# A diffusion backbone on one core: weight buffers of the whole program in place of one pool for each stage, and eight copies on another engine

## The chip, the core and the metric

The kernel runs on one core of one Trainium2 chip. The metric is the device time of one launch in microseconds (us). The kernel before has a median of 3383.81 us over three runs (3368.09 to 3385.52).

## The reference

Two layers work on 512 latent tokens `x`, and the first of them on 256 context tokens `xc` as well; the model width is 1024. Each sub-layer is modulated by vectors that come from a conditioning vector through `mod_w`. Cut to what matters here:

```python
def _swiglu(h, w1, w2):                       # 1024 -> 2 x 2816 -> 1024
    gate, up = jnp.split(h @ w1, 2, axis=-1)
    return (jax.nn.silu(gate) * up) @ w2

for l in range(2):
    x  = x  + 0.5 * ml[2] * _swiglu(_modnorm(x,  ...), ffn_w1[l, 0], ffn_w2[l, 0])
    xc = xc + 0.5 * mc[2] * _swiglu(_modnorm(xc, ...), ffn_w1[l, 0], ffn_w2[l, 0])
    hl, hc = _modnorm(x, ...), _modnorm(xc, ...)
    if l == 0: yl, yc = _mixer_ab(hl, hc, ...)   # RWKV-7 heads beside an S5 state space model, both ways
    else:      yl, _  = _mixer_c(hl, hc, ...)    # windowed attention of the latents, all context keys
    x  = x + ml[5] * yl
    x  = x + 0.5 * ml[8] * _swiglu(_modnorm(x, ...), ffn_w1[l, 1], ffn_w2[l, 1])
    # layer 0 does the same for xc
return _rmsnorm(x, final_g)
```

The S5 part needs powers 0 to 8 of a complex number for each of its 32 groups, 64 states and two directions; they are worked out once from the parameters.

## The kernel before

The arithmetic is float32 made of two reduced parts. Each weight block goes through `weight` (L340): SyncE starts a DMA of 4 x 128 rows into a raw buffer `wraw` (L351), then `split` (L316) lets ScalarE round it to the high part `wh` (L319) and VectorE subtract that from the raw block to get the low part `wl` (L320). `mm3` multiplies with three matmuls: high by high, high by low, low by high (L361 to L363). A buffer pair `wh`, `wl` holds 1024 rows of 128 columns, so a step of 256 columns takes two pairs and, for 1024 rows, two raw buffers. A raw buffer is free when its two casts and two subtractions are done; a pair is free when the matmuls that read it are done.

The tokens go through `modnorm`: VectorE writes `nt` (L332), ScalarE `hh` (L335), VectorE `hl` (L336), for 8 blocks of 128 channels. `ffn` takes 256 columns of gate and of up weights at a time (matmuls `pg`, `pu`; 96 of them for 256 tokens), ScalarE makes `sg` of `pg` (L397), and `out_blocks` adds the second product to the stream (`po`, L431).

`dit_kernel` (L1634 to L1710) writes the program in five stages, each inside `with net.weights(raw, w)`, which opens a pool of weight buffers (L103 to L108) and closes it at the stage's end:

| stage | work | raw buffers, pairs | us in the trace |
|---|---|---|---|
| A | first ffn of the context, the S5 parameters, some modulation vectors | 5, 5 | 0 to 325 |
| B | both streams of layer 0: latent ffn, mixers, context ffn | 2, 4 | 325 to 1955 |
| E | second ffn of layer 0 and first of layer 1, latents | 3, 4 | 1955 to 2724 |
| F | keys, values and queries of the attention | 2, 4 | 2724 to 2820 |
| G | attention heads, out projection, last ffn, final norm | 4, 4 | 2820 to 3377 |

Only `mix_out` of the latents, with the `ab_out` weights at the end of B, has a pool of its own (`W_M`). Buffers of a new pool that lie where those of a closed one lay can be filled only when the closed pool's last readers are done. A scheduler that simulates the program's times (`schedule_with_timeline_sim`) sets the order on every engine, SyncE's DMA starts among them; within a pool, buffers of a kind go round in turn. SyncE takes its DMAs one after the other: one that waits for its buffer holds up all behind it.

`s5_params` (L926 and on) runs beside A's ffn: VectorE works out the powers `pw` (L953), eight copies of 64 x 256 put them in the order that GpSimd wants (`pe` and `po`, L1039 to L1042, four for the real part and four for the imaginary), and GpSimd multiplies them with `sbb` and `sct` (L1088 to L1095). `sctn` (L1067) is made of the last parts of `sct`, which come from TensorE transposes (`psc`).

Of the kernel before, what the change touches and what calls it, by code (L numbers as in the profile page):

```python
# [8 lines left out]
F32 = mybir.dt.float32  # L9
I32 = mybir.dt.int32  # L10
F32R = mybir.dt.float32r
# [7 lines left out]
KB = D // 128  # L19
# [17 lines left out]
IN_L = (3, 11, 2, 1)  # L37
PS = (1, 4, 1)
AHEAD = 3000
W_B = (2, 4)  # L40
M_B = 2
M_A = 3
LATE = (3, 20)
# [4 lines left out]
F_S5 = (0.8, 1)  # L48
T_PREP = 30
T_ITEM = {1: 12, 2: 24}  # L50
W_E = (3, 4)
W_M = (2, 4)
W_F = (2, 4)
W_G = (4, 4)
P_BUFS = 7
TWO_PI = 6.283185307179586
PI_LO = 3.1415925
# [3 lines left out]
class Net:  # L61
    def __init__(self, tc, ctx, a, out):
        self.tc, self.nc, self.a, self.out = tc, tc.nc, a, out
        self.norm_bufs, self.start, self.mw, self.mp_bufs = None, False, None, 1
        self.rs, self.hook = {}, None
        e = ctx.enter_context
        self.const = e(tc.tile_pool(name="const", bufs=1))
        self.xl = e(tc.tile_pool(name="xl", bufs=1)).tile([128, KB, LAT], F32, name="xl")
        self.tp = e(tc.tile_pool(name="tp", bufs=2))
        self.dram = e(tc.tile_pool(name="dram", bufs=1, space=DRAM))  # L70
        self.pm = e(tc.tile_pool(name="pm", bufs=2, space=PSUM))

# [30 lines left out]
    @contextmanager  # L103
    def weights(self, raw, wb, side="right"):

        with self.tc.tile_pool(name="wp", bufs=2, side=side) as self.wp:
            self.bufs = (raw, wb)
            yield  # L108

    @contextmanager  # L110
    def mod_weights(self, n, side="right"):
# [228 lines left out]
    def weight(self, ap, pool=None, bufs=None, wide=256):  # L340

        nc = self.nc
        _, kk, n = ap.shape
        pool, (rb, wb) = (pool, bufs) if pool else (self.wp, self.bufs)
        res = [tuple(pool.tile([128, KB, 128], F32R, tag=f"w{p}", bufs=wb, name=f"w{p}") for p in "hl")
               for _ in range(0, n, 128)]
        for k0 in range(0, kk, 4):
            ks = slice(k0, min(kk, k0 + 4))
            raw = pool.tile([128, 4, max(n, wide)], F32, tag="w", bufs=rb, name="wraw")
            r = raw[:, :ks.stop - k0, :n]  # L350
            nc.sync.dma_start(out=r, in_=ap[:, ks, :])  # L351
            for j, (hi, lo) in enumerate(res):
                self.split(hi[:, ks, :], lo[:, ks, :], r[:, :, j * 128:(j + 1) * 128])
        return res
# [571 lines left out]
    def s5_params(self, pool):  # L926

        nc, a = self.nc, self.a
# [20 lines left out]
        dt = small("dt")  # L949
        for d in range(2):  # L950
            nc.gpsimd.dma_start(out=dt[64 * d:64 * d + 64, :], in_=a["s5_log_step"][0, d].partition_broadcast(64))
        V = nc.vector
# [34 lines left out]
        pw = pool.tile([128, 9, 2, 32], F32, tag="spw", bufs=1, name="pw")  # L987
# [48 lines left out]
        pe = pool.tile([128, 2, 8, 32], F32, tag="spe", bufs=1, name="pe")  # L1036
        po = pool.tile([128, 2, 8, 32], F32, tag="spo", bufs=1, name="po")
        for ri in range(2):
            V.tensor_copy(pe[0:64, ri], pw[0:64, 7::-1, ri, :])  # L1039
            V.tensor_copy(pe[64:128, ri], pw[64:128, 0:8, ri, :])  # L1040
            V.tensor_copy(po[0:64, ri], pw[0:64, 1:9, ri, :])
            V.tensor_copy(po[64:128, ri], pw[64:128, 8:0:-1, ri, :])  # L1042

        bt = pool.tile([128, 2, 33, 16], F32, tag="sb", bufs=1, name="sb")
        bb = pool.tile([128, 2, 33, 16], F32, tag="sbb", bufs=1, name="sbb")
# [409 lines left out]
    def final(self, grp):  # L1455

        nc = self.nc
        c0, n = grp
        ps = [[self.dense("pf") for _ in range(2)] for _ in range(n // 128)]
        for k in range(KB):  # L1460
            xs = self.xs(k, grp)
            nc.scalar.activation(out=xs, in_=xs, func=ACTF.Copy, scale=self.vec["final_g"][:, k:k + 1])
            for t, p in enumerate(ps):
                nc.tensor.transpose(p[k // 4][:, k % 4 * 128:(k % 4 + 1) * 128], xs[:, t * 128:(t + 1) * 128], self.ident)
        y = self.token_rstd(grp, self.norm_psum())
        for t, p in enumerate(ps):
            for hf in range(2):
                ob = self.wp.tile([128, 512], F32, tag="w", bufs=self.bufs[0], name="ob")
                if hf:
                    nc.vector.tensor_scalar(out=ob, in0=p[hf], scalar1=y[:, t:t + 1], scalar2=None, op0=ALU.mult)  # L1470
                else:
                    nc.scalar.activation(out=ob, in_=p[hf], func=ACTF.Copy, scale=y[:, t:t + 1])
                nc.sync.dma_start(out=self.out[0, c0 + t * 128 - CTX:c0 + (t + 1) * 128 - CTX, hf * 512:hf * 512 + 512], in_=ob)
# [42 lines left out]
def dit_kernel(ctx: ExitStack, tc: tile.TileContext, args, out):  # L1516
# [117 lines left out]
    xs = ctx.enter_context(ExitStack())  # L1634
    net.xc = xs.enter_context(right("xc")).tile([128, KB, CTX], F32, name="xc")
    with net.psum(*PS), left("mix") as mp:
        with net.mod_weights(M_A), net.weights(5, 5), right("r1") as rp:
            net.setup()
            net.start = True
            net.mod_vectors(rp)  # L1640
            run(net.load_x(args["ctx"][0], net.xc, rp))
            for k in range(KB):
                net.sq_add(k, G_CTX)
            with net.mod_weights(M_0, "left"):
                run(mods(0, 0, 1))
            net.start = False

            def more():
                yield LATE[1]
                with left("l1") as lp:  # L1650
                    net.s5_params(lp)
                net.vectors(rp)
                net.rwkv_setup(mp)
                yield from net.load_x(args["x"][0], net.xl, rp)
                for grp in LATS:
                    for k in range(KB):
                        net.sq_add(k, grp)
                        yield 2
            weave(ffn(0, 0, C, rp, FF_A), (late(LATE[0], mods(0, 2, 3, 4)), F_MOD), more())
        with net.mod_weights(M_B), net.weights(*W_B):  # L1660
            weave(ctx_stream(), lat_stream(), (chain(mods(0, 5, 6, 7, 8), mods(1, 0, 1, 2, 3, 4, 5)), 8.5))
    kp = ctx.enter_context(left("kv"))
    with net.psum(0, 2, m=4):
# [25 lines left out]
    with net.psum(0, 2, 0, 2):  # L1689
        late_w = ctx.enter_context(ExitStack())  # L1690
        with left("at") as ap:
            h = tuple(ap.tile([128, KB, LAT], F32R, tag=f"h{p}", bufs=1, name=f"h{p}") for p in "hl")
            with left("ah") as hp:
                units, first = [(i, g) for g in range(4) for i in range(LAT // 128)], []
                with net.weights(*W_F), left("aq") as qp:
                    hv = {g: tuple(x[:, :, g[0] - CTX:g[0] - CTX + g[1]] for x in h) for g in LATS}
                    run(norm(1, 1, LATS, hv), net.attn_kv(LATS, hv, qp))
                    q = net.attn_q(h, ap, qp)
                    for _ in range(3):
                        next(q)  # L1700
                    run(net.attn_scores(*units[0], first, hp), q)
                m = tuple(ap.tile([128, KB, LAT], F32R, tag=f"h{p}", bufs=1, name=f"m{p}") for p in "hl")
                late_w.enter_context(net.weights(*W_G))
                run(net.attn_heads(units, first, m, hp))
            run(net.mix_out(net.a["attn_out_w"][0], LATS, m, net.modv[1, 5]))
# [46 lines left out]
```

## Time and profile before

| what | value |
|---|---|
| median of three runs | 3383.81 us (3368.09 to 3385.52) |
| the profiled execution's own time | 3378.99 us |
| its span in the trace | 3377.3 us |
| mean granted TensorE clock | 0.975 of full speed |
| TensorE busy | 3231.3 us, 96% |
| VectorE busy | 1929.3 us, 57% |
| ScalarE busy | 1330.0 us, 39% |
| GpSimd busy | 330.2 us, 10% |

A row of a timeline gives an instruction's start and duration, the engine, the line in the kernel, the operation, what it writes and reads, how many stand together, and in square brackets how long the engine had been idle before it and what ended that. "<-DVE xc L431" is read as: the engine had to wait for what VectorE wrote on line 431. Lines are those of the kernel before.

### The profile page before, as it was taken

What the parts mean: (1) busy time and instruction counts of PE and PEld (TensorE: products, weight loads), DVE (VectorE), ACT (ScalarE), POOL (GpSimd) and SP (SyncE); (2) the same over time, 40 slices, a digit from 0 to 9 for tenths busy, and PEclk for the clock granted to TensorE, in tenths of its full rate; (3) what the DMA queues carried; (4) which work ended last, traced back from release to release, by engine and by line L of the source; (5) the groups of instructions that cost most, each with busy time, mean ns of one, the idle gap of its engine ahead of it and who ended that gap; (6) DMA issues with size and microseconds to landing.
All of it is one profiled execution on the core that took longest, in us unless ns stands there. A gap on an engine that the chain in (4) does not pass through costs nothing.

```text
span 3377.3 us, 63691 instructions
## 1 busy us (share of the span) xinstructions
PE 3231.3 (96%) x25549; PEld 2787.6 (83%) x25549; DVE 1929.3 (57%) x4281; ACT 1330.0 (39%) x2709; POOL 330.2 (10%) x489
## 2 busy tenths in 40 slices
PE   7899999999998989999999899999999999999999
PEld 5788888987897878888888888888888886698888
DVE  4786656445458788558666553335433377663334
ACT  3334444223245555333334442224322256552224
POOL 2690000400000024500000000000000000000000
PEclk8999999989998999999999999999999999999999
DMA  9657555434334656653544542334433232033321
GB/s 305 224 192 213 155 161 174 155 111 142 103 100 146 192 187 219 187 166 92 155 132 153 172 137 94 100 100 144 135 100 97 94 91 66 1 125 100 100 97 66
DMA packets 448385, 462.95 MB, mean 137 GB/s; under 512 B 72638, under 2 KB 410458, under 8 KB 448090
## 3 DMA queue, kind: packets, MB, share of 16 engines
q1 hardware_dynamic: 446560, 457.04, 42.7%
q8 instruction: 201, 3.29, 0.4%
q0 software_dynamic: 704, 1.16, 0.2%
q10 hardware_dynamic: 826, 0.68, 0.1%
q14 instruction: 94, 0.77, 0.1%
HBM read 422.71 MB, written 35.55 MB: 136 GB/s over the span
## 4 chain that ended last, share of the span: by engine, by line
PE 76%; DMA 10%; DVE 7%; ACT 3%; issue 1%; SPq 1%; POOL 1%; DVEq 0%; ACTq 0%; POOLq 0%
PE po L361 7%; PE po L362 6%; PE po L363 6%; PE pu L362 6%; PE pu L361 6%; PE pg L361 6%; PE pg L362 6%; PE pu L363 6%; PE pg L363 6%; DMA wraw<-in_ffn_w_dram 4%; DVE wl L320 3%; PE psn L216 2%; PE py L858 2%; PE pgr L777 1%; DMA wraw<-in_ab_in_w_dram 1%; ACT wh L319 1%
## 5 line engine op out<-in xcount | busy, mean ns | idle before, releaser
L319 ACT CAST wh<-wraw 128x512 fp32r<-128x512 f32 (+1 forms) x1172 | 660.4, 600 | 1360.6 <-PE pu L362 297.4
L320 DVE TENSOR_TENSOR wl<-wraw,wh 128x512 fp32r<-128x512 f32 (+1 forms) x1172 | 800.1, 709 | 535.3 <-ACT wh L319 526.1
L361 PE MATMUL po<-ah,wh 128*128 128x256 f32 (+1 forms) x1520 | 483.9, 321 | 22.2 <-DVE xc L431 11.2
L361 PE MATMUL pg<-hh,wh 128*128 128x256 f32 (+1 forms) x1456 | 473.6, 325 | 18.0 <-ACT wh L319 9.0
L362 PE MATMUL po<-al,wh 128*128 128x256 f32 (+1 forms) x1520 | 476.5, 315 | 2.3 <-DVE al L320 2.3
L363 PE MATMUL po<-ah,wl 128*128 128x256 f32 (+1 forms) x1520 | 474.9, 314 | 0.0
L363 PE MATMUL pg<-hh,wl 128*128 128x256 f32 (+1 forms) x1456 | 470.4, 323 | 2.1 <-DVE wl L320 2.1
L362 PE MATMUL pg<-hl,wh 128*128 128x256 f32 (+1 forms) x1456 | 470.6, 323 | 1.0 <-DVE hl L336 0.8
L361 PE MATMUL pu<-hh,wh 128*128 128x256 f32 (+1 forms) x1456 | 469.9, 323 | 1.4 <-ACT wh L319 1.4
L362 PE MATMUL pu<-hl,wh 128*128 128x256 f32 (+1 forms) x1456 | 469.6, 323 | 0.0
L363 PE MATMUL pu<-hh,wl 128*128 128x256 f32 (+1 forms) x1456 | 467.8, 321 | 0.7 <-DVE wl L320 0.7
L361 PEld LDWEIGHTS po<-ah,wh 128*128 128x128 f32 x1520 | 288.5, 191 | 64.4 <-DVE xc L431 14.2
L361 PEld LDWEIGHTS pg<-hh,wh 128*128 128x128 f32 x1456 | 280.4, 193 | 48.1 <-ACT wh L319 12.1
L362 PEld LDWEIGHTS po<-al,wh 128*128 128x128 f32 x1520 | 290.4, 191 | 24.0 <-DVE al L320 3.8
L363 PEld LDWEIGHTS po<-ah,wl 128*128 128x128 f32 x1520 | 290.0, 191 | 17.6 <-issue 0.7
L362 PEld LDWEIGHTS pg<-hl,wh 128*128 128x128 f32 x1456 | 280.3, 193 | 27.3 <-DVE hl L336 3.4
L363 PEld LDWEIGHTS pg<-hh,wl 128*128 128x128 f32 x1456 | 280.2, 192 | 26.2 <-DVE wl L320 3.6
L361 PEld LDWEIGHTS pu<-hh,wh 128*128 128x128 f32 x1456 | 279.7, 192 | 24.5 <-issue 2.2
L362 PEld LDWEIGHTS pu<-hl,wh 128*128 128x128 f32 x1456 | 279.6, 192 | 22.1 <-issue 2.3
L363 PEld LDWEIGHTS pu<-hh,wl 128*128 128x128 f32 x1456 | 279.1, 192 | 22.4 <-DVE wl L320 1.5
L431 DVE SCALAR_TENSOR_TENSOR xl<-po,mod,xl 128x256 f32<-128x256 f32 (+1 forms) x240 | 131.9, 552 | 233.0 <-PE po L363 231.9
L398 DVE TENSOR_TENSOR sg<-sg,pu 128x512 f32<-128x512 f32 x121 | 82.8, 684 | 267.9 <-PE pu L363 267.7
(424 smaller groups left out, 5055.2 us busy)
## 6 DMA issues: line engine op xcount, KB each, us to landing
wraw<-in_ffn_w_dram SPq DMA_DIRECT2D x436, 512.0 KB, 4.4
wt<-in_mod_w_dram SPq DMA_DIRECT2D x144, 512.0 KB, 4.9
wraw<-in_ab_in_w_dram SPq DMA_DIRECT2D x72, 256.0 KB, 3.5
wraw<-in_ffn_w_dram SPq DMA_DIRECT2D x52, 256.0 KB, 3.3
arbk<-arbk SPq DMA_DIRECT2D x24, 512.0 KB, 3.0
wraw<-in_ab_out_w_dram SPq DMA_DIRECT2D x24, 512.0 KB, 3.6
ebtl<-ebt SPq DMA_DIRECT2D x16, 512.0 KB, 3.4
ab<-arbk SPq DMA_DIRECT2D x16, 512.0 KB, 4.4
```

Of the source, the lines that this page charges most:

```text
L216: nc.tensor.matmul(ps[32 * q:32 * q + 32, :256], self.sc[:, k0 + i, :], wt[:, 256 * q:256 * q + 256], start=k0 + i == 0, stop=k0 + i == KB ...
L319: nc.scalar.copy(out=hi, in_=src)
L320: nc.vector.tensor_tensor(out=lo, in0=src, in1=hi.bitcast(F32), op=ALU.subtract)
L361: nc.tensor.matmul(ps, wh, xh, start=first, stop=False)
L362: nc.tensor.matmul(ps, wh, xl, start=False, stop=False)
L363: nc.tensor.matmul(ps, wl, xh, start=False, stop=last)
L398: nc.vector.tensor_tensor(out=sg, in0=sg, in1=pu, op=ALU.mult)
L431: nc.vector.scalar_tensor_tensor(out=xs, in0=ps[:, :n], scalar=gate[:, k, gi:gi + 1], in1=xs, op0=ALU.mult, op1=ALU.add)
L777: nc.tensor.matmul(pg[:, o:o + 128], ab[hs, e, 4 + 2 * c:6 + 2 * c, :], ab[hs, e, c:4:2, :], start=True, stop=True)
L858: nc.tensor.matmul(py2[64 * hh:64 * hh + 64, o:o + 64], lhs, rhs, start=n < 2, stop=n >= len(steps) - 2, tile_position=(0, 64 * hh))
```

## The change

`self.wp` becomes a pool that is open for the whole program, with two raw buffers and four pairs (`W_BASE`). `weights` no longer replaces it: in A it opens a second pool with 3 raw buffers and 1 pair more, in E with 1 raw buffer more, in G with 2 more; B and F open none. A new function `wtile` hands out buffers in turn, first those of the base and then those of the second pool. The number of buffers in each stage is what it was; those of the base are no longer closed at a border. `weight` and `final` use `wtile`. Besides, the eight copies of `s5_params` are issued to ScalarE.

```diff
-W_B = (2, 4)
+W_BASE = (2, 4)
-W_E = (3, 4)
+W_A = (3, 1)
+W_E = (1, 0)
-W_F = (2, 4)
-W_G = (4, 4)
+W_G = (2, 0)
+        self.wp = e(tc.tile_pool(name="wb", bufs=2))
+        self.more, self.wturn = (None, 0, 0), [0, 0, 0]
     def weights(self, raw, wb, side="right"):
-        with self.tc.tile_pool(name="wp", bufs=2, side=side) as self.wp:
-            self.bufs = (raw, wb)
+        with self.tc.tile_pool(name="wp", bufs=2, side=side) as wp:
+            self.more = (wp, raw, wb)
             yield
+            self.more = (None, 0, 0)
+    def wtile(self, tag, shape, dt, i, name):
+        (wp, *more), base = self.more, W_BASE[i > 0]
+        n = self.wturn[i] % (base + more[i > 0])
+        self.wturn[i] = (n + 1) % (base + more[i > 0])
+        pool, bufs = (self.wp, base) if n < base else (wp, more[i > 0])
+        return pool.tile(shape, dt, tag=tag, bufs=bufs, name=name)
...
-            raw = pool.tile([128, 4, max(n, wide)], F32, tag="w", bufs=rb, name="wraw")
+            raw = new("w", [128, 4, max(n, wide)], F32, 0, "wraw")
...
-            V.tensor_copy(pe[0:64, ri], pw[0:64, 7::-1, ri, :])
-            V.tensor_copy(pe[64:128, ri], pw[64:128, 0:8, ri, :])
-            V.tensor_copy(po[0:64, ri], pw[0:64, 1:9, ri, :])
-            V.tensor_copy(po[64:128, ri], pw[64:128, 8:0:-1, ri, :])
+            nc.scalar.copy(out=pe[0:64, ri], in_=pw[0:64, 7::-1, ri, :])
+            nc.scalar.copy(out=pe[64:128, ri], in_=pw[64:128, 0:8, ri, :])
+            nc.scalar.copy(out=po[0:64, ri], in_=pw[0:64, 1:9, ri, :])
+            nc.scalar.copy(out=po[64:128, ri], in_=pw[64:128, 8:0:-1, ri, :])
...
-        with net.mod_weights(M_A), net.weights(5, 5), right("r1") as rp:
+        with net.mod_weights(M_A), net.weights(*W_A), right("r1") as rp:
-        with net.mod_weights(M_B), net.weights(*W_B):
+        with net.mod_weights(M_B):
-                with net.weights(*W_F), left("aq") as qp:
+                with left("aq") as qp:
```

Since the scheduler's simulation sees other buffers, it also writes another order. Three places follow. In the S5 parameters, before, VectorE has in a row (`xc` is the context stream that A's `po` is added to):

```order
L953 TENSOR_TENSOR pw<-pw,tw 128x4x32
L431 SCALAR_TENSOR_TENSOR xc<-po,mod_2_340,xc 128x256
L954 TENSOR_SCALAR a_779<-pw 128x32
L1034 COPY a_779<-pw 128x32
L1039 COPY pe<-pw 64x256
L1040 COPY pe<-pw 64x256
L1041 COPY po<-pw 64x256
L1042 COPY po<-pw 64x256
L431 SCALAR_TENSOR_TENSOR xc<-po,mod_2_340,xc 128x256
L320 TENSOR_TENSOR wl<-wraw,wh 128x512
```

Now VectorE has there (the lines of the changed kernel are 12 to 15 higher):

```order
L968 TENSOR_TENSOR pw<-pw,tw 128x4x32
L969 TENSOR_SCALAR a_782<-pw 128x32
L1049 COPY a_782<-pw 128x32
L446 SCALAR_TENSOR_TENSOR xc<-po,mod_2_343,xc 128x256 x2
L332 TENSOR_TENSOR wl<-wraw,wh 128x512
```

And ScalarE, in the same place:

```order
L331 CAST ah<-sg 128x512
L1054 COPY pe<-pw 64x256
L1055 COPY pe<-pw 64x256
L1056 COPY po<-pw 64x256
L1057 COPY po<-pw 64x256
L1054 COPY pe<-pw 64x256
L1055 COPY pe<-pw 64x256
L1056 COPY po<-pw 64x256
L1057 COPY po<-pw 64x256
L331 CAST wh<-wraw 128x512
```

The four copies of the imaginary part no longer stand on VectorE ahead of the second `xc`, and on ScalarE all eight stand ahead of four casts of weights.

At the border from A to B, SyncE (`wt` are modulation weights, `wa` small RWKV weights) has before:

```order
L351 DMA wraw<-in_ffn_w_dram 128x4x256 x7
L213 DMA wt<-in_mod_w_dram 128x1024 x6
L351 DMA wraw<-in_ab_in_w_dram 128x4x128
L582 DMA wa_4489<-in_rwkv_w_dram 64x2x128
L582 DMA wa_4489<-in_rwkv_a_dram 64x2x128
L351 DMA wraw<-in_ffn_w_dram 128x4x256 x2
```

Now it has:

```order
L366 DMA wraw<-in_ffn_w_dram 128x4x256 x7
L225 DMA wt<-in_mod_w_dram 128x1024 x2
L366 DMA wraw<-in_ffn_w_dram 128x4x256
L225 DMA wt<-in_mod_w_dram 128x1024
L366 DMA wraw<-in_ffn_w_dram 128x4x256
L225 DMA wt<-in_mod_w_dram 128x1024
L366 DMA wraw<-in_ffn_w_dram 128x4x256
L225 DMA wt<-in_mod_w_dram 128x1024
L366 DMA wraw<-in_ffn_w_dram 128x4x256
L366 DMA wraw<-in_ab_in_w_dram 128x4x128
```

The first four raw blocks of B's first ffn step stand between the last modulation weights of A instead of behind them and behind the first block of `ab_in`.

At the border from B to E, SyncE has before:

```order
L351 DMA wraw<-in_ffn_w_dram 128x4x256 x12
L351 DMA wraw<-in_ab_out_w_dram 128x4x256 x2
L213 DMA wt<-in_mod_w_dram 128x1024 x2
L351 DMA wraw<-in_ab_out_w_dram 128x4x256 x14
L351 DMA wraw<-in_ffn_w_dram 128x4x256 x3
```

Now it has:

```order
L366 DMA wraw<-in_ffn_w_dram 128x4x256 x12
L366 DMA wraw<-in_ab_out_w_dram 128x4x256 x2
L366 DMA wraw<-in_ffn_w_dram 128x4x256
L366 DMA wraw<-in_ab_out_w_dram 128x4x256 x14
L366 DMA wraw<-in_ffn_w_dram 128x4x256
```

One of E's blocks now stands between the `ab_out` blocks, and three more stand further ahead: the group that ends with these 12 had 12 blocks of ffn weights and now has 15. At E to F, SyncE's order of `attn_in` blocks and of the small DMAs behind them is as it was; ScalarE casts four of their blocks ahead of the norm. At F to G, three blocks of `attn_out` now stand among the last 24 `rsw` DMAs (the rotation of the queries, L1303), the first of them ahead of 20, where all 16 stood behind them. Inside B the order differs at many places, with the same instructions.

## Rows read from the trace of the kernel before

**Rows 1.** The page, part 1: busy time, share of the span, number of instructions.

```profile
PE 3231.3 (96%) x25549; PEld 2787.6 (83%) x25549; DVE 1929.3 (57%) x4281; ACT 1330.0 (39%) x2709; POOL 330.2 (10%) x489
```

**Rows 2.** Stretches: length, busy PE, PEld, DVE, ACT, POOL; granted clock, DMA share, GB/s.

```profile
300.00:350.00 50.00, 42.98 (x333) 38.90 (x332) 32.75 (x91) 22.32 (x47) 0.61 (x2) 0.86 0.55 170
330.00:340.00 10.00, 5.24 (x21) 4.65 (x22) 8.71 (x30) 6.56 (x14) 0.00 (x0) 0.50 0.67 204
350.00:1930.00 1580.00, 1514.36 (x15252) 1349.65 (x15252) 989.86 (x2435) 651.72 (x1337) 172.95 (x323) 0.97 0.49 152
1930.00:1980.00 50.00, 42.93 (x346) 40.15 (x345) 34.73 (x78) 26.34 (x53) 0.00 (x0) 0.93 0.54 179
2720.00:2760.00 40.00, 31.62 (x222) 29.45 (x222) 32.49 (x80) 23.43 (x52) 0.00 (x0) 0.87 0.29 89
```

**Rows 3.** Timeline of VectorE, S5 parameters: start, duration, line, what, [idle before].

```profile
103.47 1.39 DVE L1039 COPY pe<-pw 64x256 f32<-64x256 f32 x1
104.87 1.82 DVE L1040 COPY pe<-pw 64x256 f32<-64x256 f32 x1
106.72 0.28 DVE L1041 COPY po<-pw 64x256 f32<-64x256 f32 x1
107.02 3.74 DVE L1042 COPY po<-pw 64x256 f32<-64x256 f32 x1
...
111.19 5.49 DVE L320 TENSOR_TENSOR wl<-wraw,wh 128x512 fp32r<-128x512 f32 x4
```

**Rows 4.** Timeline of TensorE, S5 parameters.

```profile
102.91 0.39 PE L361 MATMUL po<-ah,wh 128*128 128x256 f32 x1 [1.40 <-DVE xc L431]
...
105.05 0.28 PE L363 MATMUL po<-ah,wl 128*128 128x256 f32 x1
...
111.33 0.58 PE L361 MATMUL po<-ah,wh 128*128 128x256 f32 x1 [5.88 <-DVE xc L431]
```

**Rows 5.** Timeline of GpSimd, S5 parameters.

```profile
129.80 1.56 POOL L1067 TENSOR_SCALAR sctn<-sct 128x512 f32<-128x512 f32 x1 [12.16 <-ACT sct L1056]
```

**Rows 6.** Timeline of ScalarE, S5 parameters.

```profile
115.19 1.36 ACT L319 CAST wh<-wraw 128x512 fp32r<-128x512 f32 x2 [8.79 <-issue]
```

**Rows 7.** ScalarE's own copies of 64 x 256 (ns: least, median, most).

```profile
L1341 ACT CAST kh<-kro x16: 402/405/408, 2749.3 to 2767.4; 64x256 fp32r<-64x256 f32 x16
...
L1207 ACT COPY xn<-se x24: 611/635/653, 779.4 to 1700.7; 64x256 f32<-64x256 f32 x24
```

**Rows 8.** Timeline of SyncE's queue, border from A to B.

```profile
311.71 13.37 SPq L213 DMA_DIRECT2D wt<-in_mod_w_dram  x6
326.39 0.38 SPq L351 DMA_DIRECT2D wraw<-in_ab_in_w_dram  x1
...
328.23 1.14 SPq L351 DMA_DIRECT2D wraw<-in_ffn_w_dram  x2
```

**Rows 9.** Timeline of VectorE, border from A to B.

```profile
326.89 0.89 DVE L336 SCALAR_TENSOR_TENSOR hl<-nt,mod,hh 128x256 fp32r<-128x256 f32 x2
```

**Rows 10.** Timeline of TensorE, border from A to B.

```profile
333.50 0.58 PE L361 MATMUL pg<-hh,wh 128*128 128x256 f32 x1 [4.26 <-ACT wh L319]
```

**Rows 11.** Timeline of ScalarE, border from A to B: B's first `sg`.

```profile
347.68 0.58 ACT L397 ACTIVATE sg<-pg 128x512 f32<-128x512 f32 x1
```

**Rows 12.** Timeline of SyncE's queue, border from B to E.

```profile
1954.17 1.47 SPq L351 DMA_DIRECT2D wraw<-in_ffn_w_dram  x3
```

**Rows 13.** Timeline of TensorE, border from B to E.

```profile
1960.80 0.58 PE L361 MATMUL pg<-hh,wh 128*128 128x256 f32 x1 [3.50 <-ACT wh L319]
```

**Rows 14.** Timeline of ScalarE, border from B to E: E's first `sg`.

```profile
1973.99 0.60 ACT L397 ACTIVATE sg<-pg 128x512 f32<-128x512 f32 x1
```

**Rows 15.** Timeline of SyncE's queue, attention.

```profile
2723.96 14.87 SPq L351 DMA_DIRECT2D wraw<-in_attn_in_w_dram  x6
...
2780.89 33.98 SPq L1303 DMA_DIRECT2D rsw<-qt  x24
```

**Rows 16.** Timeline of TensorE, border from E to F.

```profile
2730.62 0.80 PE L361 MATMUL pkv<-hh,wh 128*128 128x256 f32 x2 [1.62 <-ACT hh L335]
```

More of the change, by code (lines that the diff above doesn't have):

```diff
@@ L343, in weight @@
         _, kk, n = ap.shape
-        pool, (rb, wb) = (pool, bufs) if pool else (self.wp, self.bufs)
-        res = [tuple(pool.tile([128, KB, 128], F32R, tag=f"w{p}", bufs=wb, name=f"w{p}") for p in "hl")
-               for _ in range(0, n, 128)]
+        if pool:
+            rb, wb = bufs
+            new = lambda tag, shape, dt, i, name: pool.tile(shape, dt, tag=tag, bufs=wb if i else rb, name=name)
+        else:
+            new = self.wtile
+        res = [tuple(new(f"w{p}", [128, KB, 128], F32R, 1 + i, f"w{p}") for i, p in enumerate("hl")) for _ in range(0, n, 128)]
         for k0 in range(0, kk, 4):
             ks = slice(k0, min(kk, k0 + 4))
-            raw = pool.tile([128, 4, max(n, wide)], F32, tag="w", bufs=rb, name="wraw")
+            raw = new("w", [128, 4, max(n, wide)], F32, 0, "wraw")
             r = raw[:, :ks.stop - k0, :n]
@@ L1467, in final @@
             for hf in range(2):
-                ob = self.wp.tile([128, 512], F32, tag="w", bufs=self.bufs[0], name="ob")
+                ob = self.wtile("w", [128, 512], F32, 0, "ob")
                 if hf:
```

## The prediction

> **What bounds the kernel now.** First the page: TensorE is busy for 96% of the span [rows 1], so nothing that another engine saves counts by itself; only time in which TensorE stands still, or runs at its lower clock level, can be won. Then the stretches [rows 2], to see where that time lies. Each border between two stages is short of work: 7.0 us of the 50 from A to B (50 less 42.98), 7.1 of the 50 from B to E, 8.4 of the 40 from E to F. The long stage B misses 65.6 of its 1580, spread thin. The granted clock falls with them: in the ten microseconds from 330 it is 0.50, the 1.2 GHz level, with TensorE busy for only 5.24 of them behind a wait [rows 2, 10]. Last the timelines at the S5 parameters and at the borders, to see what ended each wait. The reader should look there for the bracket behind TensorE's first matmul of each piece of work.
>
> **Eight copies leave VectorE.** The second four take 1.39 + 1.82 + 0.28 + 3.74 = 7.23 us [rows 3]; they stand between one `xc` and the next, and TensorE waits 5.88 us for that `xc`, after 1.40 us for the one before [rows 4]. The 0.28 us copy is the same instruction as the 3.74 us one, while GpSimd works on its own products beside them. The wait of 5.88 is one for VectorE's order, not for work that `xc` needs. Without the copies it falls to what an addition and its PSUM bank cost, which I put at under 1 us, and the 1.40 us shrinks somewhat.
>
> On ScalarE eight such copies cost between 8 x 0.405 = 3.2 us and 8 x 0.635 = 5.1 us [rows 7]. I take 3.2, since the cheaper row is the same plain copy of 64 x 256 between buffers. They stand ahead of four weight casts, and then VectorE's four `wl`, 5.49 us for four beside GpSimd [rows 3], come later too. The cover is ScalarE's idle time, 8.79 us ahead of the cast at 115.19 [rows 6]; if the casts are needed at once there is none, and the 3.2 to 5.1 us come back as a wait for `wh`. Of the 7.28 us of waits I take **5** as won, with 0 (the late weights eat all of it) and 7.3 as ends. What is queued behind the copies on ScalarE is these casts and a copy of `sct`. GpSimd waits for `sctn` at 129.80 anyway, after 12.16 us without work [rows 5], so its own chain gains nothing from earlier copies.
>
> The Trainium skill ("ScalarE: Activation LUTs", section "Rules for kernel authors") speaks against this half: for simple element-wise work it says to use VectorE, not ScalarE, since VectorE is faster per element. By that rule, at 0.28 us against 0.405, the move would lose 8 x 0.125 = 1.0 us, and the sum would be 6 us poorer. The trace disagrees here, since the copies beside GpSimd averaged 1.81 us. Another page explains the disagreement: "SBUF — State Buffer", section "Who interferes with whom", says that VectorE and GpSimd share a pair of ports that one of them holds for a whole instruction, and that ScalarE has ports of its own. By it the 3.2 us are not stretched on ScalarE; no run here shows that for this place.
>
> **Border A to B.** Before, the first raw blocks of B's ffn are taken by SyncE at 328.23, behind six modulation weights that hold the queue from 311.71 on and behind the first block of `ab_in` [rows 8]; TensorE waits 4.26 us and starts at 333.50 [rows 10]. Now four blocks stand among the modulation weights, and ScalarE casts them among the last squares of A. The next late thing is the norm: the first two `hl` end at 326.89 + 0.89 = 327.8 [rows 9]. From there 96 matmuls go before the first `sg`. The pace is 18 matmuls from 102.91 to 105.05, 2.14 / 17 = 0.126 us each [rows 4], so 96 take 12.1 us; with a short sum for the other norm between them the first `sg` comes near 340.5 instead of 347.68 [rows 11]. I take **7**, with 3 (only the wait of 4.26, less one block that is still late) and 9 (7.0 idle plus what the clock gives back) as ends. The six modulation weights come later by four blocks; nobody waits for them in A. The `ab_in` block moves behind the four and is used later than they are.
>
> **Border B to E.** The first three blocks of E leave SyncE at 1954.17 [rows 12], TensorE waits 3.50 us until 1960.80 [rows 13], and the first `sg` is at 1973.99 [rows 14]. Now four blocks are taken earlier, three of them ahead of all of `ab_out` and one among it. Half of the casts go ahead of the norm, and VectorE runs `nt` and `hl` without eight `wl` between. The 3.50 us go, and a part of the thinner waits behind it (7.1 us in the whole window): **4.5**, ends 1 and 7. A block that waits for a raw buffer would hold `ab_out` behind it: that is why the lower end is this low.
>
> **Border E to F.** SyncE's order is the same, but its six `attn_in` blocks, which took the queue from 2723.96 for 14.87 us [rows 15], no longer wait for a new pool, and four of eight casts go ahead of the norm. TensorE's wait at 2730.62 was for `hh`, not for a weight [rows 16], so the norm stays in front: **2**, ends 0 and 4.
>
> **F to G.** Three `attn_out` blocks now stand among the last 24 `rsw`, which took 33.98 us of the queue [rows 15], 1.42 us each. Early weights spare ScalarE a burst of casts in the softmax: **1**. The upper end is 3. The lower one is bounded by the same row: each of the three may hold the next eight rotations for as long as eight take, 11.3 us, so -34.
>
> **Inside B** the count of buffers is the same, and the order differs without a pattern. The stage has 65.6 us of thin waits [rows 2]; a difference of an eighth of them either way is 8 us, and I take 0.
>
> Sum: 5 + 7 + 4.5 + 2 + 1 = 19.5 us. The profiled execution took 3378.99 us, of which 3377.3 are the span; less 19.5 that gives 3359.5, about **3360**. The median of the runs shown is 4.8 us higher than the profiled run, inside their spread of 17 us, and I leave the forecast on the profiled one. With the smaller and larger ends taken together in part, the forecast's own range is 3352 to 3368.
>
> **Rivals.** (a) Half of it is covered by something else. For it: the late casts after the copies, GpSimd's wait for `sctn` [rows 5], and the norm, which is the next late thing at three borders. Against it: the waits named were plainly for `xc` and for a DMA [rows 4, 8, 10]. S5 gives 0, A to B 5, B to E 3, the rest nothing: 3379 - 8 = 3371.
>
> (b) The borders keep their waits: the base buffers are still held by the old stage's last matmuls, so a block that is asked for earlier arrives no earlier. Against it stands the queue, which was idle between the six modulation weights and the first block only by their transfer. Then only the copies count: 3379 - 5 = 3374.
>
> (c) The clock comes back as well. With no wait of 3 us or more at a border TensorE may stay at 2.4 GHz, where it showed 0.50 for ten microseconds from 330 [rows 2]. All upper ends with 4 from B: 7.3 + 9 + 7 + 4 + 3 + 4 = 34.3, so 3345.
>
> (d) Slower: a weight block at the head of SyncE's queue. The mechanism is F to G: an `attn_out` block waits for one of the two raw buffers of the base, which come free only when `attn_in` weights have been cast into pairs that TensorE still reads, and behind it eight rotations wait, and behind these the scores. Price 3 x 11.3 = 34 us; with all the other gains it gives 3378.99 - 18.5 + 34 = 3394, with those of (a) 3379 - 8 + 34 = 3405. It makes the kernel slower from 18.5 us on, that is from 6.2 us for each of the three. For it: the queue takes its DMAs in order. Against it: raw buffers come free at the cast, well ahead of the matmuls, and the simulation that wrote the order counts the same buffers.
>
> **How the numbers follow.** A measurement of this kernel can tell about 0.5%, 17 us, from no change; faster means under 3367, slower over 3401. Chances: forecast 0.45, (a) 0.25, (b) 0.06, (c) 0.11, (d) 0.13. The forecast's range lies nearly all below 3367: with (c) and a little of (a) faster has 0.53. (b), most of (a) and the milder half of (d) are within 0.5%: 0.38. Slower keeps 0.09. The range leaves out the far part of (c) and that of (d) beyond 3388: 3340 to 3388.
>
> **What would show it.** On the changed kernel's timelines: the copies on ScalarE at 0.40 us each, and TensorE's 5.88 us wait near 111 gone. The first `pg` of B right behind the norm's first `hl`, with an `sg` some 7 us earlier than before counted from A's last `po`. The wait ahead of E's first `pg` under 1 us. A granted clock above 0.50 in the ten microseconds after A. Against it: TensorE's waits near 106 now put down to `wh` or `wl` (then the S5 term is 0); SyncE's queue with a block that waits for a buffer in front of `rsw` or `ab_out` (then (d)); and idle TensorE time in B well over 65.6 us, which would say that the new order inside the stage, which I set at nothing, is the larger term.

## The result and the profile after

The changed kernel takes 3361.46 us (median of 20 runs, 3350.80 to 3377.21); the kernel before takes 3382.66 us beside it (20 runs). The two medians lie 21.2 us apart; the ratio taken over all runs, which is the one with an interval, is 0.9947, 95% interval 0.9933 to 0.9961: 17.9 us or 0.53% less. 3360 us had been forecast, and faster by over 0.5% as the likeliest case. The total came out; most of its terms did not, as the rest of this document shows. The profiled execution of the changed kernel happens to be a long one, with a span of 3372.3 us, so its span says less than its stages do.

The page and the windows of the changed kernel, part 1 and the same stretches as [rows 1, 2] (length, busy PE, PEld, DVE, ACT, POOL; granted clock, DMA share, GB/s):

```profile
PE 3231.2 (96%) x25549; PEld 2780.2 (82%) x25549; DVE 1919.3 (57%) x4273; ACT 1333.1 (40%) x2717; POOL 334.9 (10%) x489
```

```profile
300.00:350.00 50.00, 42.72 (x329) 35.17 (x328) 36.12 (x104) 22.45 (x49) 0.61 (x2) 0.93 0.61 194
350.00:1930.00 1580.00, 1507.06 (x15202) 1346.38 (x15202) 983.67 (x2426) 652.16 (x1337) 175.09 (x323) 0.96 0.49 153
1930.00:1980.00 50.00, 45.16 (x364) 41.94 (x363) 30.68 (x70) 22.95 (x47) 0.00 (x0) 0.97 0.36 121
2720.00:2760.00 40.00, 36.14 (x241) 33.69 (x242) 33.44 (x81) 23.62 (x56) 0.00 (x0) 0.91 0.23 67
```

In these two traces stage A ends 13 us earlier (7 us in the second pair of traces; the other 6 lie ahead of the S5 parameters), so the windows do not cover the same work, and a stretch has to be measured between two events of the program. The table does that: each number is the time from the start of one row of the trace to the start of another. For a kernel that was traced twice both numbers stand.

| us from ... to ... | before (twice) | copies alone | buffers alone | changed (twice) |
|---|---|---|---|---|
| S5 parameters: A's third `sg` to its fourth | 56.8, 56.8 | 48.8 | 56.5 | 48.7, 48.7 |
| rest of A: fourth `sg` to A's last `xc` | 183.9, 184.5 | 187.5 | 183.9 | 184.8, 184.8 |
| A to B: A's last `xc` to B's first `sg` | 21.3, 21.5 | 21.2 | 18.0 | 20.2, 17.9 |
| B: its first `sg` to its last `xl` | 1606.5, 1603.4 | 1613.7 | 1603.4 | 1612.9, 1608.7 |
| B to E: B's last `xl` to E's first `sg` | 19.8, 19.4 | 19.9 | 18.8 | 18.5, 18.4 |
| E: its first `sg` to its last `xl` | 750.0, 750.1 | 750.0 | 749.3 | 751.9, 750.0 |
| E to F: E's last `xl` to F's first `kvt` | 18.6, 18.6 | 18.2 | 15.2 | 15.2, 15.0 |
| F and scores: that `kvt` to the last `pS` | 200.5, 200.4 | 200.0 | 198.2 | 196.1, 197.8 |
| out projection and norm: the last `pS` to `sg` number 100 | 69.7, 69.7 | 69.6 | 71.3 | 72.2, 72.2 |
| last ffn: `sg` number 100 to the last, number 121 | 313.8, 313.0 | 313.9 | 321.5 | 321.9, 321.0 |

Places of 20 to 70 us repeat within 0.5 us in most rows; A to B of the changed kernel does not. Nor does stage B, as the second experiment shows. The last row is a loss of 8 us that no step of the forecast had.

### The profile page after: what moved, and what is told of

The parts are those of the page before. It is cut to its first block, busy times and chain, and to the rows that moved or that the text cites. A ratio compares the mean times of both kernels' runs of the same rounds, so it can differ in the third digit from the quotient of the medians.

```text
span 3372.3 us, 63687 instructions
## 1 busy us (share of the span) xinstructions
PE 3231.2 (96%) x25549; PEld 2780.2 (82%) x25549; DVE 1919.3 (57%) x4273; ACT 1333.1 (40%) x2717; POOL 334.9 (10%) x489
## 4 chain that ended last, share of the span: by engine, by line
PE 70%; DMA 11%; DVE 10%; ACT 4%; POOL 2%; issue 2%; SPq 1%; DVEq 0%; ACTq 0%; POOLq 0%
PE po L376 6%; PE pg L376 6%; PE pg L377 6%; PE pg L378 5%; PE po L378 5%; PE po L377 5%; PE pu L378 5%; PE pu L377 5%; PE pu L376 5%; DMA wraw<-in_ffn_w_dram 5%; DVE wl L332 4%; DMA wt<-in_mod_w_dram 2%; PE py L873 2%; ACT wh L331 2%; PE pgr L792 1%
## 5 line engine op out<-in xcount | busy, mean ns | idle before, releaser
L376 PEld LDWEIGHTS pg<-hh,wh 128*128 128x128 f32 x1456 | 278.2, 191 | 49.3 <-ACT hh L347 14.8
```

The lines of the kernel that those rows point to most:

```text
L376: nc.tensor.matmul(ps, wh, xh, start=first, stop=False)
```

## Experiments

### The two halves, and both kernels once more

Four kernels on one chip. `before_again` and `after_again` are unchanged. `e1_pool_only` is the changed kernel with its eight copies back on VectorE; `e2_copies_only` is the kernel before with the copies on ScalarE:

```diff
-            V.tensor_copy(pe[0:64, ri], pw[0:64, 7::-1, ri, :])
+            nc.scalar.copy(out=pe[0:64, ri], in_=pw[0:64, 7::-1, ri, :])
...
```

> The changed kernel once more, for a second trace and for its time beside the parts. Both theories: about 0.995 of the kernel before. If the gains at single places of the first trace (13 us by the end of stage A, 1 us from A to B, a loss of 5 us inside B, 3 to 4 us each at E to F and F to G) belong to the order of the instructions, they stand here within 1 us each; where they belong to one execution, they move.

> The kernel before once more, for a second trace of it. Ratio 1.000 within its interval. The waits of 5.88 us at the S5 parameters and of 4.26 and 3.50 us at the borders stand again. In the two traces at hand a matmul of 512 columns in the last ffn starts every 227 ns before and every 234 ns after, at the same granted clock: if that is of the execution and not of the kernel, it may stand at either value here.

> The changed kernel with the eight copies back on VectorE: only the weight buffers are changed. Theory (the two halves add up, copies about 7 us at the S5 parameters, buffers the rest): ratio to before about 0.997, the waits for xc near 105 us stand again, the gains at E to F and F to G stay. Rival (nearly all is the copies, the buffers only shuffle waits): ratio 0.999 to 1.001. Second rival (the copies do nothing, since the order that the scheduler writes with the new buffers is what helps stage A): 0.995 and no wait near 105.

> The kernel before with the eight copies on ScalarE: one pool for each stage, as before. Theory: the 5.88 us wait is gone, about 7 us of stage A saved, ratio to before about 0.998. Rival (nearly all is the copies): 0.995 to 0.996. Second rival (copies do nothing): 1.000, with a wait for wh or wl in place of the one for xc.

Measured: after_again 0.9963 (0.9943 to 0.9983), before_again 0.9994 (0.9969 to 1.0019), buffers alone 0.9971 (0.9956 to 0.9986), copies alone 1.0002 (0.9981 to 1.0022). So the buffers alone are shown to be faster, and the copies alone are not. Of the first trace's gains S5, B to E and E to F stand again in the second; A to B moved from 1.2 us to 3.5, and the 13 us by the end of A to 7.

The S5 place answers cleanly. With the buffers alone TensorE's timeline has the wait of [rows 4] again. With the copies alone it is gone, and the only wait for an `xc` left there is a short one, ahead of a later matmul:

```profile
105.07 0.58 PE L376 MATMUL po<-ah,wh 128*128 128x256 f32 x1 [5.90 <-DVE xc L446]
```

```profile
109.78 0.39 PE L361 MATMUL po<-ah,wh 128*128 128x256 f32 x1 [0.31 <-DVE xc L431]
```

The copies themselves, in the changed kernel's ScalarE timeline, against [rows 3]:

```profile
93.84 0.41 ACT L1054 COPY pe<-pw 64x256 f32<-64x256 f32 x1 [4.44 <-DVE pw L968]
...
96.78 0.40 ACT L1057 COPY po<-pw 64x256 f32<-64x256 f32 x1
97.21 0.93 ACT L331 CAST wh<-wraw 128x512 fp32r<-128x512 f32 x2
```

Eight copies take 3.3 us from 93.84 on, none stretched, while GpSimd's products start at 94.74 beside them:

```profile
94.74 1.11 POOL L1103 TENSOR_TENSOR seb<-pe,sbb 128x512 f32<-128x512 f32 x1 [2.56 <-ACT pe L1055]
95.81 1.11 POOL L1103 TENSOR_TENSOR sob<-po,sct 128x512 f32<-128x512 f32 x1
```

The Trainium skill ("SBUF — State Buffer", section "Who interferes with whom") says that ScalarE's ports are not shared with GpSimd; these 0.40 us copies agree.

So the copies are worth 8.0 us at their place. In the whole time they could not be seen here: 1.0002 on the old pools, and 0.9963 with them against 0.9971 without on the new ones. Their trace gives back 3 us in the rest of A (187.5 against 183.9 and 184.5); the changed kernel gives back less than 1 (184.8). What is left goes under in stage B, whose length moves by more than the effect from one execution of a program to the next.

### The pace of back-to-back matmuls

The last ffn is nothing but matmuls of 512 columns, with TensorE busy all the time and the clock granted in full, before and after. Yet 50 us hold 222 of them in the kernel before and 216 in the changed one. Windows of the kernel before (its second trace) and of the changed one, columns as above:

```profile
3050.00:3100.00 50.00, 50.00 (x222) 41.45 (x221) 18.76 (x30) 13.89 (x26) 0.00 (x0) 1.00 0.33 106
```

```profile
3050.00:3100.00 50.00, 50.00 (x216) 40.23 (x215) 17.13 (x27) 13.34 (x24) 0.00 (x0) 1.00 0.32 105
```

From start to start a matmul takes 226.7 ns there before and 233.3 ns after. This is the same in both traces of either kernel and in the trace of the buffers alone, so it belongs to the program. What the change moved is where things lie. From the built programs, the place of activations and weights within 128 bytes of a partition:

```
stage, pool           before: activations, weights   changed: activations, weights
A        r1              96, 96                         96, 64 (one pair of five 96)
B latent lf              96, 96                         96, 64
B context cf              0, 96                          0, 64
E        l12             64, 64                         64, 64
G        r7              96, 96                         96, 64
```

Two kernels move only that. `e3_pad` is the changed kernel with 32 unused bytes ahead of the pool `r7`, which puts its activations at 64; `e4_before_pad` is the kernel before with the same edit:

```diff
-    with net.psum(0, 2, m=4), right("r7") as rp:
+    with net.psum(0, 2, m=4), right("r7p") as rq, right("r7") as rp:
+        rq.tile([128, 8], F32, tag="pad", bufs=1, name="pad")
```

> The changed kernel with 32 unused bytes a partition ahead of the last ffn's pool, so that activations and weight buffers there start at the same place within 128 bytes; before the change they did, with the change they are 32 bytes apart. Theory (the pace of back-to-back matmuls hangs on that): the 1344 matmuls of 512 columns of the last ffn start every 227 ns instead of 234, 8 to 9 us less from the first of them to the last, those of 256 columns every 120 instead of 117; ratio to the kernel before about 0.993. Rival (it hangs on where the weights lie in the memory, or on what else runs): 234 stays and the ratio is that of the changed kernel, 0.995 to 0.996.

> The kernel before with the same 32 bytes ahead of the last ffn's pool: there they move activations and weights apart. Theory: 234 ns in place of 227 in the last ffn, 9 us more, ratio 1.002 to 1.003. Rival: 227 stays, ratio 1.000.

Measured: e3_pad 0.9899 (0.9884 to 0.9914), e4_before_pad 1.0016 (1.0001 to 1.0030). The stretch of the last row of the table takes 312.8 us in e3_pad and 322.2 in e4_before_pad, as expected; e3_pad's whole time came out below the 0.993 expected. Their windows:

```profile
3050.00:3100.00 50.00, 50.00 (x222) 41.43 (x221) 18.56 (x30) 12.99 (x24) 0.00 (x0) 1.00 0.26 85
```

```profile
3050.00:3100.00 50.00, 50.00 (x216) 40.30 (x215) 17.64 (x28) 14.87 (x27) 0.00 (x0) 1.00 0.29 94
```

The same pace can be read row by row, in TensorE's timeline of the changed kernel (0.23 from start to start) and of e3_pad:

```profile
3100.17 0.40 PE L376 MATMUL po<-ah,wh 128*128 128x512 f32 x1
3100.40 0.40 PE L377 MATMUL po<-al,wh 128*128 128x512 f32 x1
3100.64 0.40 PE L378 MATMUL po<-ah,wl 128*128 128x512 f32 x1
3100.87 0.39 PE L376 MATMUL po<-ah,wh 128*128 128x512 f32 x1
```

```profile
3100.06 0.39 PE L377 MATMUL po<-al,wh 128*128 128x512 f32 x1
3100.28 0.39 PE L378 MATMUL po<-ah,wl 128*128 128x512 f32 x1
3100.51 0.39 PE L376 MATMUL po<-ah,wh 128*128 128x512 f32 x1
3100.74 0.39 PE L377 MATMUL po<-al,wh 128*128 128x512 f32 x1
```

32 bytes move it both ways, in both kernels, and the four kernels have all four pairings of 64 and 96: the place of the one relative to the other counts. The loss of 8 us in the last ffn is the place of the new pool, and the rival (where in the memory the weights lie) falls. With 256 columns it is the other way round. In the traces at hand, the median from start to start is 120 ns for those that start at the same place, and 117 ns for those apart (118 for the context's). The new pool might therefore gain in A and B some of what it lost in G. `e8_align_ab` takes that gain away, and runs beside e3 once more and `e9_pad_dve`, which is e3 with the copies on VectorE:

```diff
-        with net.mod_weights(M_A), net.weights(*W_A), right("r1") as rp:
+        with right("pa") as ra, net.mod_weights(M_A), net.weights(*W_A), right("r1") as rp:
+            ra.tile([128, 8], F32, tag="pad", bufs=1, name="pada")
...
-        with net.mod_weights(M_B):
+        with right("pb") as rb, net.mod_weights(M_B):
+            rb.tile([128, 8], F32, tag="pad", bufs=1, name="padb")
```

> e3_pad once more, beside the two that differ from it by one thing each. Theory: 0.990 to 0.994 again, 227 ns in the last ffn. If the 0.990 was a lucky draw of stage B, nearer to 0.994.

> e3_pad with 32 more unused bytes ahead of the pools of stage A and of stage B, so that activations and weights start at the same place within 128 bytes there too, as they did in the kernel before. Theory (with 256 columns it is the other way round than with 512: apart is 117, together 120): the matmuls of A's ffn and of the latents' ffn in B start every 120 ns, and 4452 of them at 2.7 ns cost up to 12 us, less what waits hide; ratio of this to e3_again about 1.002 to 1.0035. Rival (the pace of 256 columns is hidden behind casts and transfers): same time as e3_again within 0.1%.

> e3_pad with the eight copies back on VectorE. Theory (the copies on ScalarE are worth the 8 us that they save at the S5 parameters, less some 3 us by the end of stage A): 5 us slower than e3_again. Rival (stage B gives all of it back): the same time as e3_again.

Measured: e3_again 0.9927 (0.9912 to 0.9943), e8_align_ab 0.9951 (0.9937 to 0.9965), e9_pad_dve 0.9956 (0.9939 to 0.9974). In e8's trace the matmuls of A and of the latents' ffn come every 120 ns, in e3_again's every 117 to 118. The price is 0.9951 / 0.9927 = 1.0024, about 8 us, inside what was expected, but the two intervals overlap (0.9937 to 0.9943): it is likely, not shown. In A the pace is worth nothing that can be seen, since e8 takes as long there as e3_again (48.8 and 48.7 us at S5, 184.6 and 185.9 in the rest); what there is of it must lie in B. The copies are worth 0.9956 / 0.9927 = 1.0029 here; by the medians of the two kernels it is 3361.57 - 3355.99 = 5.6 us. That fits the 5 us expected, but these intervals overlap too, and with the 1.0002 above it is likely rather than shown. In VectorE's timeline of e9_pad_dve the copies take what they took in [rows 3]:

```profile
98.18 1.39 DVE L1054 COPY pe<-pw 64x256 f32<-64x256 f32 x1
99.59 1.82 DVE L1055 COPY pe<-pw 64x256 f32<-64x256 f32 x1
101.44 0.28 DVE L1056 COPY po<-pw 64x256 f32<-64x256 f32 x1
101.74 3.74 DVE L1057 COPY po<-pw 64x256 f32<-64x256 f32 x1
```

e3_pad and e3_again are one program. Their whole times, 0.9899 and 0.9927, differ as much as the two prices just read, so e8 and e9 are set against e3_again, which ran beside them, and not against e3_pad. Their traces show how little one trace says of stage B: 1602.1 us in one, 1622.4 in the other, mostly in this window, at a granted clock of 0.97 and of 0.94:

```profile
1340.00:1900.00 560.00, 523.06 (x5723) 468.28 (x5722) 342.78 (x866) 219.98 (x451) 46.06 (x95) 0.97 0.48 146
```

```profile
1340.00:1900.00 560.00, 528.46 (x5641) 470.58 (x5639) 332.14 (x846) 210.88 (x433) 45.98 (x95) 0.94 0.47 139
```

### The border from A to B

The forecast of 7 us came to 1.2 and 3.5. The blocks of B's ffn did come early. In the kernel before, the first `pg` starts 7.1 us after A's last addition (333.50 in [rows 10] against 326.35). In the changed kernel it waits 2.51 us and starts at 316.21, 2.9 us after the last addition, which is the second of the two `xc` in this row and starts at 313.27:

```profile
326.35 0.48 DVE L431 SCALAR_TENSOR_TENSOR xc<-po,mod,xc 128x256 f32<-128x256 f32 x1 [0.45 <-PE po L363]
```

```profile
312.88 0.87 DVE L446 SCALAR_TENSOR_TENSOR xc<-po,mod,xc 128x256 f32<-128x256 f32 x2
316.21 0.39 PE L376 MATMUL pg<-hh,wh 128*128 128x256 f32 x1 [2.51 <-ACT hh L347]
```

But from there to the first `sg` TensorE goes slowly. In this first trace the clock falls as well, to 0.78 from 320 to 330 us, where the second trace keeps 1.00 and is 2.3 us shorter at this border:

```profile
320.00:330.00 10.00, 7.75 (x40) 6.71 (x41) 7.82 (x39) 2.72 (x6) 0.00 (x0) 0.78 0.45 138
```

```profile
320.00:330.00 10.00, 7.85 (x56) 6.83 (x56) 8.17 (x40) 3.02 (x7) 0.00 (x0) 1.00 0.41 128
```

ScalarE's and SyncE's timelines show one suspect:

```profile
321.85 0.91 ACT L347 ACTIVATE hh<-nt,mod 128x256 fp32r<-128x256 f32 x2 [1.47 <-DVE nt L344]
325.89 0.62 ACT L331 CAST wh<-wraw 128x512 fp32r<-128x512 f32 x1 [3.13 <-DMA wraw<-in_ab_in_w_dram]
326.42 0.91 ACT L347 ACTIVATE hh<-nt,mod 128x256 fp32r<-128x256 f32 x2
333.43 0.60 ACT L412 ACTIVATE sg<-pg 128x512 f32<-128x512 f32 x1 [6.10 <-PE pg L378]
```

```profile
320.45 7.18 SPq L366 DMA_DIRECT2D wraw<-in_ab_in_w_dram  x2
```

The second block of `ab_in` can only be fetched when the first has left the one raw buffer that these weights have, and its cast stands on ScalarE ahead of the norm's last two `hh`. `e6_ab_raw2` gives it a second buffer:

```diff
-        w, = self.weight(..., pool, (1, self.ibufs[3]), 128)
+        w, = self.weight(..., pool, (2 if self.ibufs is IN_C else 1, self.ibufs[3]), 128)
```

> e3_pad with two raw buffers instead of one for the blocks of ab_in of the context stream. At the border from A to B ScalarE has the cast of ab_in's second block ahead of two blocks of the norm, and waits 1.8 to 3.1 us for that block's transfer, which starts only when the first block's buffer is free. Theory (this wait is what kept the border from giving the forecast 7 us): from A's last xc to B's first sg it takes 14.5 to 16 us instead of 17.9 to 20.2. Rival (the norm itself and the low clock set the border): 17.5 or more as before. The rest of stage B gets another order, so the whole time says little: 0.990 to 0.997.

Measured: 0.9962 (0.9948 to 0.9976), and 19.0 us from A's last `xc` to B's first `sg`. ScalarE's wait for `ab_in` is gone, and the border is no shorter: the rival holds. Its VectorE timeline shows what probably sets it. The eight `hl` come one by one between `wl`, `nt` and the small steps of the other norm:

```profile
315.23 0.87 DVE L348 SCALAR_TENSOR_TENSOR hl<-nt,mod,hh 128x256 fp32r<-128x256 f32 x2
...
319.89 0.47 DVE L348 SCALAR_TENSOR_TENSOR hl<-nt,mod,hh 128x256 fp32r<-128x256 f32 x1
...
322.56 0.48 DVE L348 SCALAR_TENSOR_TENSOR hl<-nt,mod,hh 128x256 fp32r<-128x256 f32 x1
...
325.11 0.47 DVE L348 SCALAR_TENSOR_TENSOR hl<-nt,mod,hh 128x256 fp32r<-128x256 f32 x1
```

From the first to the last it takes 325.11 - 315.23 = 9.9 us, and after that the last blocks' matmuls are still to do, then comes the other norm's copy on ScalarE. The early weights are there; VectorE, which makes the norm and half of each weight, is the next late thing, as far as rows can say: no run made the norm any faster. The whole of e6 is longer than e3 by its stage B (1620.4 us), which, by the two traces above, says nothing on the buffer.

### The border from B to E

Here the forecast of 4.5 us came to about 1.2. One of E's blocks leaves SyncE only at B's very end, ScalarE waits for it, and TensorE's first `pu` for ScalarE. SyncE, ScalarE and TensorE of the changed kernel:

```profile
1946.36 0.37 SPq L366 DMA_DIRECT2D wraw<-in_ffn_w_dram  x1
```

```profile
1952.30 1.66 ACT L331 CAST wh<-wraw 128x512 fp32r<-128x512 f32 x3 [4.14 <-DMA wraw<-in_ffn_w_dram]
```

```profile
1952.97 0.39 PE L376 MATMUL pu<-hh,wh 128*128 128x256 f32 x1 [2.64 <-ACT wh L331]
```

1946.36 is the start of B's last `xl`. In the built program this block goes to the one raw buffer that stage E adds with a pool of its own (`W_E = (1, 0)`), and that buffer lies where `ab_out`'s weights lay: it is a stage's pool still. `e10_e_base` is e3 without it:

```diff
-        with net.weights(*W_E, "left"), net.mod_weights(2), left("l12") as lp:
+        with net.mod_weights(2), left("l12") as lp:
```

> e3_pad without the second pool of stage E: two raw buffers there, both of the base, instead of three. At the border from B to E the third raw block of E, the first half of the first up weights, falls to the one buffer of the stage's own pool, lies where buffers of ab_out lay, and starts only at B's last xl; ScalarE waits 4.1 us for it. Theory (that buffer is why the border gained 1 us and not 4.5): from B's last xl to E's first sg 14.5 to 16.5 us instead of 18.3. Rival (the norm sets it): 17.5 or more. Stage E itself (750 to 752 us from first sg to last xl): the same if two raw buffers do there, up to 5 us longer if not. Whole time 0.989 to 0.993.

Measured: 14.45 us from B's last `xl` to E's first `sg`, as expected, against 18.3 to 18.5; E itself takes 750.0 us, so two raw buffers do there. The whole time is 0.9923 (0.9892 to 0.9954), which cannot be told from e3's 0.9899 and 0.9927. In its trace neither TensorE nor ScalarE waits for a weight of E at the border.

The border from E to F was not tried apart. Its gain stands in every trace: 14.8 to 15.5 us in the nine with the base pool, 18.0 to 18.6 in the four without.

## Why the prediction was right, and where not

**The copies**: 5 us forecast, 8.0 measured at the place, above the upper end of 7.3. The wait of 5.88 us is gone, as forecast. The term was mis-sized because TensorE's matmuls behind that wait, which ran at the lower clock (0.50 from 111 to 114 us), had been left out, and a third wait, of 1.33 us, for the next `xc`. ScalarE's idle time covered the copies at 0.40 us each. With the copies alone some 3 us are given back later in A, with both halves 0.6; the forecast allowed for that only in a rival.

**A to B**: 7 forecast, 1.2 and 3.5 in the two traces (3.3 with the buffers alone). The step that failed is the one that let 96 matmuls follow the first `hl` at 0.126 us each. Weights came early as it said; but the first `pg` came 2.9 us behind the last `xc`, not 1.5, and from it to the first `sg` it took 15.0 and 17.2 us, not 12.7. VectorE made the eight `hl` over some 10 us, and by the rows the end of that chain, not its start, sets the first `sg`; in the first trace the low clock adds to it. That the norm is the next late thing had been seen and then not costed.

**B to E**: 4.5 forecast, 1.2 measured, 5.2 once the last stage-owned buffer was gone (14.45 against 19.4 and 19.8). The mechanism and its size were right for the base's buffers. The failed step is that it took all of E's early blocks as free, while the third of them falls to a buffer outside the base; rival (b) was true for that one buffer.

**E to F**: 2 forecast, 3.5 measured; all eight casts stand ahead of the norm's first `hh`, where four did. **F to G**: 1 forecast, 2 to 4 by the table. How much of that is the pool's is open: e4_before_pad, which has the old pools, takes 197.5 us in that row.

Rival (d), rotations held by `attn_out` blocks, came true on a small scale. The first of the three blocks waits 5.3 us for VectorE's `wl` to free its raw buffer. ScalarE has the next rotations' data (`qt`) done at 2776.65, and they start behind the block at 2778.28, at most 1.6 us late, in both traces, and not 11.3. The other two blocks hold nothing: behind the third, which is shown too, the rotations wait for their `qt`. In SyncE's timeline:

```profile
2777.80 0.37 SPq L366 DMA_DIRECT2D wraw<-in_attn_out_w_dram  x1
2778.28 3.02 SPq L1318 DMA_DIRECT2D rsw<-qt  x4
...
2783.71 6.51 SPq L1318 DMA_DIRECT2D rsw<-qt  x8
2790.32 0.53 SPq L366 DMA_DIRECT2D wraw<-in_attn_out_w_dram  x1
2796.65 6.95 SPq L1318 DMA_DIRECT2D rsw<-qt  x8
```

**Left out**: the pace. It costs 8 us in the last ffn, and it likely gives about 8 us in B, by e8. The forecast held the matmuls' own time constant, as a change of buffers leaves their number and shape alone. If the price by e8 holds, the two sides nearly cancel. Another 2.5 us are lost between the scores and the last ffn's first `sg`; they stand in e3_pad too (72.1 us), so the place of the last ffn's pool is not their cause, which stays open.

Put together by the table, in the means of two traces: 8.1 at the S5 place, less 0.6 in the rest of A, 2.4 at A to B, 1.2 at B to E, 3.5 at E to F, 3.5 in F and the scores, less 2.5 behind them, less 8.0 in the last ffn: 7.6 us outside of B and E. The measured difference is 17.9 us with an interval of 13 to 23, so some 10 us must lie in B, which the forecast set at nothing. There the four traces show 6 us more and not less, and the granted clock says why they cannot be trusted. In the comparison of the two halves it was 0.9738 in the mean of 35 runs of the kernel before and 0.9781 in 12 of the changed one (copies alone 0.9737, buffers alone 0.9785). Among those 35 runs 0.001 more goes with 2.7 us less, so 0.0043 go with some 11 us. But the two traces of the kernel before have 0.975 and 0.979, above its mean, and those of the changed kernel 0.975 and 0.977, below its own. So rival (c), the clock that comes back, was true in part, and by the buffers. Whether the clock is the cause, or follows from shorter waits inside B, and how much of it is the pace, these runs cannot part.

**Of the whole**: the right number came from a sum of which two terms were too large and three too small, and which lacked a loss of 8 us in the last ffn and, by the whole times, a gain of some 10 in B. The mechanisms at S5 and at B to E are shown by experiments, the gains at the other borders stand in the traces, and the range held; that its middle came so near is luck.

## What to carry to other kernels

A buffer that outlives a stage takes only its own wait away: look which of the next stage's first blocks really falls to it (here the third did not), and what makes the other operand of the first matmul. A change of pools moves every address behind it; compare the matmuls per 50 us in a stretch that TensorE fills, before and after, since the busy share and the granted clock do not show a slower pace. Small copies of an engine that shares its time with the critical path are dear by what they are queued in front of, not by their own length.

The best version here is the changed kernel with 32 unused bytes ahead of the last ffn's pool, 0.9899 and 0.9927 of the kernel before in two comparisons.

## What the hardware showed that was not expected

Back-to-back matmuls of 128 x 128 weights with changing weights run at two paces at the same granted clock, 2.4 GHz, and the place of activations and weights decides. Same place within 128 bytes: 226.7 ns for 512 columns and 120 ns for 256. Apart: 233.3 ns for 512 columns (by 32 bytes), and 117 to 118 ns for 256 (by 32 or 64). So 512 columns want the same place and 256 columns want another. It holds in all traces looked at, with places of 0, 64 and 96; why, and whether a wider unit than 128 bytes counts (the pairs that agreed here agree within 1024 bytes too), was not tried.

Four copies of 64 x 256 took VectorE 1.39, 1.82, 0.28 and 3.74 us, to within 0.02 in the traces looked at, and ScalarE 0.40 us each time. GpSimd's timeline of the kernel before, beside them:

```profile
103.39 1.32 POOL L1065 TENSOR_TENSOR sbb<-sbb,sgt 128x512 f32<-128x512 f32 x1
104.65 0.74 POOL L1053 DMA_DIRECT2D scl<-in_s_c_im_dram  x1
105.41 1.11 POOL L1088 TENSOR_TENSOR sob<-po,sct 128x512 f32<-128x512 f32 x1
106.45 0.74 POOL L1053 DMA_DIRECT2D scl<-in_s_c_im_dram  x1
107.22 1.11 POOL L1089 TENSOR_TENSOR sox<-pe,sbb 128x512 f32<-128x512 f32 x1
108.28 1.10 POOL L1088 TENSOR_TENSOR seb<-pe,sbb 128x512 f32<-128x512 f32 x1
109.33 1.26 POOL L1091 TENSOR_TENSOR seb<-seb,sox 128x512 f32<-128x512 f32 x1
```

The copy of 0.28 us at 106.72 [rows 3] falls between two products, where GpSimd only starts a DMA. The other three end at 104.86, 106.69 and 110.76, each 0.15 to 0.17 us after a product ends (104.71, 106.52, 110.59), and the longest lasts through three products on end. But the copy of 1.82 us, too, begins while GpSimd only starts a DMA. That GpSimd is the cause is argued from these rows; no run took GpSimd's work away.
